# The S5 kernel matrix of a hybrid decoder block, stored with the group outside

## The chip, the cores and the metric

One core of a Trainium2 chip runs the whole block in one launch. The metric is the device time of that launch in microseconds (us). The kernel before took 2400.34 us, the median of three runs (2392.76 to 2401.52).

## The reference, cut to what matters

The block has two parallel heads behind a modulated RMSNorm (an S5 state-space group and a sparse-attention group), an output projection and a gated MLP. Only the S5 part is touched. With `u` of shape (1, 512, 1024) in float32:

```
uf = u.reshape(bsz, seq, 64, 16)                 # 64 groups of 16 channels
dt = exp(log_dt); ab = exp(lam * dt)             # complex, 64 states a group
bb = f * b                                       # f from ab and lam
bu = einsum('bsgh,gph->sbgp', uf, bb)            # complex
states = associative_scan(a * s + bu)            # over the 512 positions
y = Re(einsum('sbgp,ghp->bsgh', states, c)) + d_skip * uf
z = gelu(y); out = z * sigmoid(z @ w_glu + b_glu)
```

The kernel computes the scan in chunks of 8 positions: 512 positions are 64 chunks (index `j`), each with 8 offsets (index `l`). Inside a chunk the output is a product with a small matrix that depends only on the distance between two offsets, the S5 kernel; what comes from earlier chunks goes through a state that is scanned over the 64 chunks.

## The kernel before, in words

The work is tiled in 128 partitions by 512 positions. Phase A multiplies the input with the first weight slices; phase B1 (`phase_b1`) runs twelve further projections (`proj`, 48 matmuls each in three float32 parts), and among them eight *octets* (`s5_octet`), each the S5 work for 8 of the 64 groups. Then come attention, the GLU, the output projection and the MLP.

In an octet VectorE builds the tables `w1`, `TT`, `C`, `Sn`; TensorE transposes `w1` into `W1` (L567, copied by ScalarE at L568) and multiplies the 8 x 16 columns of the S5 kernel (L575). ScalarE copies these into `Kt` (L577): 16 partitions (the input channel `i`) by 1024 elements, stored as `x g` with `x` = 16 times the distance plus the output channel, and the group `g` inside, so that the copy writes every eighth element. VectorE adds `d_skip` at the last 16 `x` (L580). POOL's DMA queue stores `Kt` to the DRAM tensor `k_s` (L581), where a row is 15 x 128 elements: 1024 of the matrix and 896 zeros, which one DMA fills during phase A (L278). A second DMA of POOL (L585) reads the rows back shifted, row `i` for offset `l` from element 128 `l` on, 1024 contiguous elements for each of the 128 partitions. That makes the block-triangular matrix `w3`, in the profile the tile s5w; there is one buffer of it.

Meanwhile a row of the weights is multiplied with a shift vector (s5wt, L593, loaded by SP's queue) for the bias of `U` (tile s5U, L601 to L604). TensorE multiplies `W1` with `U` (L608), VectorE scans over the chunks (L615 to L618), TensorE swaps halves with a constant matrix (L621), and VectorE finishes the state `SS` (L624 to L626). At the end stands what the prediction calls the Y block, for each of the 8 groups one matmul with `w3[:, :, g]` (L630) and one with `TT[:, g]` (L631), both 64 columns wide and into one accumulator. ScalarE applies gelu (L634) and POOL stores the result to `z_d` (L635).

```
for g in range(8):
    T.matmul(Y[:, 64 * g:64 * g + 64], w3[:, :, g], U[:, g], start=True, stop=False)
    T.matmul(Y[:, 64 * g:64 * g + 64], TT[:, g, 0:8].rearrange("p k h -> p (k h)"), SS[:, g, 0:64],
             start=False, stop=True)
```

Each engine works off its own queue in order. No order is written out by hand: a planner lays the queues out when the program is built, from the order of the code, its priorities (`hp()` lifts the S5 work of TensorE) and estimated durations, so the matmuls of an octet stand among those of the projections.

Of the kernel before, what the change touches and what calls it, by code (L numbers as in the profile page):

```python
# [10 lines left out]
F32 = mybir.dt.float32  # L11
# [7 lines left out]
P = 128  # L19
# [32 lines left out]
class Block:  # L52
# [143 lines left out]
    def phase_a(self, hh, hl, tab, ps):  # L196


        nc, tc, a, V, A, T = self.nc, self.tc, self.a, self.V, self.A, self.T
        m, b = self.mod, self.mad  # L200
        with ExitStack() as st:
            pa = st.enter_context(tc.tile_pool(name="pa", bufs=1))
# [18 lines left out]
            with tc.tile_pool(name="s5p", bufs=1) as pp:  # L221
                pu = [ps.tile([P, S], F32, name="b", bufs=8) for _ in range(8)]
                for kt in range(KT):
                    asc = pa.tile([P, 2], F32, name="asc", bufs=4)
                    first = self.ada(1, kt, asc[:, 0:1 if kt else 2], pw, 3)
# [11 lines left out]
                    x = xt[kt]  # L237
# [23 lines left out]
            for kt in range(KT):  # L261
                ash = pa.tile([P, 1], F32, name="ash", bufs=4)
                self.ada(0, kt, ash, pw, 3)
                wh, wl = self.slices(a["wk"], kt)
                V.tensor_add(m[:, 0, kt:kt + 1], ash, b[:, 0, kt:kt + 1])
                if kt >= 8:
                    hl[kt] = tab.tile([P, S], F32R, name=f"hl{kt}")
                self.modulate(xt[kt], m[:, 1, kt:kt + 1], m[:, 0, kt:kt + 1], rb, hh[kt], hl[kt], pa)
                if kt < 8:
                    V.tensor_mul(us[kt], us[kt], rp)  # L270
                if kt == 4:
                    self.rot = tab.tile([P, 2, S], F32, name="rot")
                    nc.sync.dma_start(self.rot.rearrange("p a s -> p (a s)"), a["cons"][:, C_COS:])
                if kt == 1:

                    zero = pa.tile([P, P], F32, name="zero")
                    nc.gpsimd.memset(zero, 0.0)
                    self.after([nc.gpsimd.dma_start(  # L278
                        self.k_s.rearrange("o i x -> (o i) x")[:, 1024:].rearrange("p (a b) -> p a b", b=P),
                        zero.unsqueeze(1).to_broadcast([P, 7, P]))], first)  # L280
                if 2 <= kt < 10:
                    nc.sync.dma_start(self.u_d[kt - 2].rearrange("l p j -> p l j"), us[kt - 2])
                h = hh[kt], hl[kt]
                for i in range(4):
                    self.mm3(pk[i], (wh[:, i], wl[:, i]), h, kt == 0, kt == KT - 1)
                v = [w[:, 4:8].rearrange("p a m -> p (a m)") for w in (wh, wl)]
                for t in range(4):
                    self.mm3(pk[4 + t], [x[:, P * t:P * t + P] for x in h], v, kt == 0, kt == KT - 1)
            def tmp(n):
                return pw.tile([P, 2048], F32, name="adw", bufs=3)[:, 0:S * n].rearrange("p (a s) -> p a s", s=S)  # L290

            for i in range(4):
                p = pk[i]
                if i == 0:
                    q, t = (pa.tile([P, 8, 64], F32, name="modt", bufs=2).rearrange("p a b -> p (a b)")
                            for _ in range(2))
                    p = self.rope(p, q, t, self.rot[:, 0], self.rot[:, 1], 64)
                if i % 2 == 0:
                    o = tmp(4).bitcast(F32R)
                self.spill(self.qk_d[0, P * i:P * i + P], p, o[:, 2 * (i % 2):2 * (i % 2) + 2])  # L300
            o = tmp(4)
# [188 lines left out]
    def s5_octet(self, o, Tb, W, ps):  # L490

        nc, V, A, T, a = self.nc, self.V, self.A, self.T, self.a
# [3 lines left out]
        U, bc = self.s5_next  # L496
# [66 lines left out]
        with hp():  # L563
            for q in range(2):
                p = ps.tile([P, 4, P], F32, name="tp", bufs=2)
# [1 line left out]
                    T.transpose(p[:, g], w1[:, 4 * q + g].rearrange("p r i -> p (r i)"), self.ident)  # L567
                A.copy(W1[:, 4 * q:4 * q + 4], p)  # L568
        Kt = W.tile([P, 8, 9 * 16], F32, name="s5bg", bufs=3).rearrange("p a b -> p (a b)")
        Kt = Kt[:16, 0:1024].rearrange("p (x g) -> p x g", g=8)  # L570
        with hp():
            for q in range(2):
                p = ps.tile([P, 4, P], F32, name="tp", bufs=2)
                for g in range(4):
                    T.matmul(p[:16, g], bb[:, 0, 4 * q + g], TT[:, 4 * q + g, 1:9].rearrange("p k h -> p (k h)"),  # L575
                             start=True, stop=True)
                A.copy(Kt[:, :, 4 * q:4 * q + 4].rearrange("p x g -> p g x"), p[:16])  # L577
        dd = W.tile([16, 16, 8], F32, name="s5dd")
        nc.sync.dma_start(dd, a["s5d"][:, o])
        V.tensor_add(Kt[:, 112:], Kt[:, 112:], dd)  # L580
        nc.gpsimd.dma_start(self.k_s[o, :, 0:1024].rearrange("i (x g) -> i x g", g=8), Kt)  # L581
        w3 = W.tile([P, P, 8], F32, name="s5w3")

        src = self.k_s[o]
        nc.gpsimd.dma_start(w3.rearrange("p x g -> p (x g)"),  # L585
                            bass.AP(src.tensor, src.offset, [[P, 8], [15 * P, 16], [1, 1024]]))


        bu = W.tile([P, 2], F32, name="bu", bufs=2)
# [9 lines left out]
        with hp():  # L599
            p = ps.tile([P, S], F32, name="acc", bufs=4)  # L600
# [26 lines left out]
        with hp():  # L627
            Y = ps.tile([P, S], F32, name="acc", bufs=4)
            for g in range(8):
                T.matmul(Y[:, 64 * g:64 * g + 64], w3[:, :, g], U[:, g], start=True, stop=False)  # L630
                T.matmul(Y[:, 64 * g:64 * g + 64], TT[:, g, 0:8].rearrange("p k h -> p (k h)"), SS[:, g, 0:64],  # L631
                         start=False, stop=True)
            zz = W.tile([P, 8, 64], F32, name="s5x", bufs=4)
            A.activation(zz.rearrange("p g j -> p (g j)"), Y, AF.Gelu_apprx_tanh)  # L634
            nc.gpsimd.dma_start(self.z_d[o].rearrange("(h g) l j -> l h g j", g=8), zz)  # L635
# [853 lines left out]
```

## Time and profile before

| | before |
|---|---|
| median of the runs (lowest, highest) | 2400.34 us (2392.76, 2401.52) |
| the profiled execution | 2398.66 us |
| its span, first to last instruction | 2396.9 us |
| mean granted TensorE clock | 0.963 |
| TensorE matmul / weight load busy | 2244.6 us (94%) / 1967.3 us (82%) |
| VectorE, ScalarE, POOL busy | 1865.8 us (78%), 1084.3 us (45%), 288.5 us (12%) |
| DMA packets, bytes | 92370, 398.17 MB |

The busy time of TensorE counts matmuls, whose ends are modelled; weight loads run beside them and are listed apart (PEld). A float32 matmul of 128x128 weights appears as two records, so 64 matmuls of a line are "x128". [...]

### The profile page before, as it was taken

Reading aid. Unit: us, or ns where it says so; the run is one execution under the profiler, and the core shown is the slowest. Engines: PE = TensorE matmul, PEld = TensorE weight load, DVE = VectorE, ACT = ScalarE, POOL = GpSimd, SP = SyncE. Lnnn points to the kernel's source line nnn. Section 1 sums busy time; section 2 is a strip of 40 time slices with the busy share of each in tenths; the row PEclk is TensorE's granted clock in tenths of the full one; section 3 lists DMA queues with packets and bytes.
Section 4 is the critical chain, followed back from the end, with each engine's and each line's share of the span. In section 5 each row is a group of like instructions: output and inputs, shape, how many; then the busy total and the mean of one; then the engine's idle time right before and its main releaser. Section 6 shows DMA issues by size and latency. Waiting matters only on the chain.

```text
span 2396.9 us, 34691 instructions
## 1 busy us (share of the span) xinstructions
PE 2244.6 (94%) x13694; PEld 1967.3 (82%) x13694; DVE 1865.8 (78%) x2776; ACT 1084.3 (45%) x1807; POOL 288.5 (12%) x375
## 2 busy tenths in 40 slices
PE   7778999989899879899999999999999899999997
PEld 5666787866677667889999999999999788888887
DVE  7789877749988878889999999999999685433436
ACT  3322444448867742644444444444444322221215
POOL 7996110100000011000000000000000000000000
PEclk9989998979999889999999999999999999999999
DMA  9666744676576567233333333333332684323223
GB/s 339 255 223 215 235 146 140 186 207 195 174 233 218 186 251 289 101 120 119 119 119 119 119 119 119 120 119 119 119 119 102 243 322 182 139 90 126 101 88 106
DMA packets 92370, 398.17 MB, mean 166 GB/s; under 512 B 19776, under 2 KB 28352, under 8 KB 56240
## 3 DMA queue, kind: packets, MB, share of 16 engines
q1 hardware_dynamic: 77856, 344.60, 41.6%
q0 software_dynamic: 14352, 51.36, 6.1%
q8 instruction: 107, 1.75, 0.3%
q14 instruction: 55, 0.45, 0.1%
HBM read 358.20 MB, written 37.69 MB: 165 GB/s over the span
## 4 chain that ended last, share of the span: by engine, by line
PE 71%; DVE 11%; issue 6%; POOL 5%; ACT 4%; DMA 3%; SPq 0%; POOLq 0%; DVEq 0%; ACTq 0%
PE dn L88 7%; PE dn L87 7%; PE dn L89 7%; PE sa L89 7%; PE sa L87 7%; PE sa L88 7%; PE sb L87 5%; PE sb L89 5%; PE sb L88 5%; PE mm L87 2%; PE mm L89 2%; PE mm L88 2%; DVE wl L62 2%; DVE adw L111 1%; PE s L870 1%
## 5 line engine op out<-in xcount | busy, mean ns | idle before, releaser
L62 ACT CAST wh<-wr 128x1024 fp32r<-128x1024 f32 (+1 forms) x257 | 261.9, 1024 | 519.7 <-PE dn L88 331.6
L62 DVE TENSOR_TENSOR wl<-wr,wh 128x1024 fp32r<-128x1024 f32 (+1 forms) x255 | 307.2, 1209 | 68.6 <-ACT wh L62 47.7
L87 PE MATMUL dn<-ah,wh 128*128 128x512 f32 (+1 forms) x704 | 274.9, 391 | 7.6 <-ACT ah L62 7.6
L88 PE MATMUL dn<-al,wh 128*128 128x512 f32 (+1 forms) x704 | 278.0, 395 | 0.0
L89 PE MATMUL dn<-ah,wl 128*128 128x512 f32 (+1 forms) x704 | 273.3, 388 | 0.0
L1249 DVE SCALAR_TENSOR_TENSOR x<-dn,mod,x 128x512 f32<-128x512 f32 (+1 forms) x104 | 73.2, 707 | 203.4 <-PE dn L89 202.8
L87 PEld LDWEIGHTS dn<-ah,wh 128*128 128x128 f32 x704 | 132.8, 189 | 40.8 <-ACT ah L62 7.8
L89 PEld LDWEIGHTS dn<-ah,wl 128*128 128x128 f32 x704 | 132.7, 189 | 30.3
L111 DVE SCALAR_TENSOR_TENSOR adw<-adw,silc 128x2048 f32<-128x2048 f32 x63 | 147.9, 2348 | 12.1 <-DMA adw<-in_wada_dram 11.8
L88 PEld LDWEIGHTS dn<-al,wh 128*128 128x128 f32 x704 | 132.8, 189 | 29.6 <-DVE al L62 0.4
L87 PE MATMUL mm<-yh,wh 128*128 128x512 f32 (+1 forms) x320 | 130.4, 412 | 22.5 <-DVE x L1026 7.2
L62 ACT CAST wh<-wq 128x1024 fp32r<-128x1024 f32 x84 | 88.0, 1048 | 137.6 <-DVE wq L1193 101.0
L62 ACT CAST xh<-wq 128x1024 fp32r<-128x1024 f32 x84 | 88.5, 1054 | 135.8 <-DVE wq L1193 100.8
L88 PE MATMUL mm<-yl,wh 128*128 128x512 f32 (+1 forms) x320 | 129.7, 406 | 3.9 <-DVE yl L62 3.9
L1082 POOL DMA_DIRECT2D a_d<-cv x44 | 23.9, 543 | 879.4 <-DVE cv L1081 879.4
L89 PE MATMUL mm<-yh,wl 128*128 128x512 f32 (+1 forms) x320 | 129.1, 405 | 0.3 <-DVE wl L62 0.3
L62 DVE TENSOR_TENSOR wl<-wq,wh 128x1024 fp32r<-128x1024 f32 x84 | 102.4, 1220 | 33.1 <-ACT wh L62 33.1
L62 DVE TENSOR_TENSOR xl<-wq,xh 128x1024 fp32r<-128x1024 f32 x84 | 102.5, 1220 | 31.4 <-ACT xh L62 31.4
L1193 DVE TENSOR_TENSOR wq<-wq,wr 128x1024 f32<-128x1024 f32 x84 | 102.1, 1216 | 0.1
L87 PEld LDWEIGHTS mm<-yh,wh 128*128 128x128 f32 x320 | 63.0, 199 | 37.7 <-issue 12.3
L87 PE MATMUL b<-hh,wh 128*128 128x512 f32 x192 | 67.3, 408 | 23.6 <-ACT hh L238 16.4
L62 ACT CAST xh<-wr 128x1024 fp32r<-128x1024 f32 x63 | 65.8, 1044 | 47.0 <-issue 19.9
(525 smaller groups left out, 7207.3 us busy)
## 6 DMA issues: line engine op xcount, KB each, us to landing
adw<-in_wada_dram SPq DMA_DIRECT2D x49, 1024.0 KB, 7.0
wr<-in_wup_dram SPq DMA_DIRECT2D x46, 1024.0 KB, 4.9
wq<-in_wup_dram SPq DMA_DIRECT2D x42, 1024.0 KB, 6.6
wr<-in_wdn_dram SPq DMA_DIRECT2D x40, 1024.0 KB, 4.9
wr<-in_wada_dram SPq DMA_DIRECT2D x32, 1024.0 KB, 4.9
wr<-in_wout_dram SPq DMA_DIRECT2D x16, 1024.0 KB, 5.8
adw<-in_wada_dram POOLq DMA_DIRECT2D x14, 1024.0 KB, 6.9
wr<-in_wp_dram SPq DMA_DIRECT2D x12, 1024.0 KB, 5.6
```

What stands on the lines that cost most here:

```text
L62: return self.A.copy(hi, src), self.V.tensor_sub(lo, src, hi.bitcast(F32))
L87: self.T.matmul(ps, wh, xh, start=start, stop=False)
L88: self.T.matmul(ps, wh, xl, start=False, stop=False)
L89: self.T.matmul(ps, wl, xh, start=False, stop=stop)
L111: self.V.scalar_tensor_tensor(t, t, 1.0, self.silc, op0=ALU.mult, op1=ALU.mult, accum_out=out)
L870: T.matmul(s[:, :c + n], q[hd], K[b][:, i, k0:k0 + c + n], start=i == 0, stop=i == 1)
L1082: self.nc.gpsimd.dma_start(self.a_d[:, m], val)
L1193: V.tensor_add(src, src, add)
L1249: V.scalar_tensor_tensor(x, p, self.mod[:, 5, m:m + 1], x, op0=ALU.mult, op1=ALU.add)
```

## The change

The group moves outside. In DRAM a row of `k_s` becomes 8 pieces of 240 elements, one per group: 128 of the matrix and 112 zeros. `Kt` becomes `g x`, so that the copy at L577 writes contiguous elements; the addition reads `dd` with the group rearranged. The store writes 8 pieces of 128 elements (512 bytes) in each of 16 rows in place of one of 1024. The load of `w3` reads 8 pieces of 128 elements in each of 128 partitions in place of one of 1024, and the shift from one offset `l` to the next is 16 elements. The zero fill writes 8 pieces of 112 elements in each of 128 rows in place of 7 x 128. The weight tile of L630 is `w3[:, g]`, 128 contiguous elements a partition.

```
-                    zero = pa.tile([P, P], F32, name="zero")
+                    zero = pa.tile([P, 112], F32, name="zero")
...
-                        self.k_s.rearrange("o i x -> (o i) x")[:, 1024:].rearrange("p (a b) -> p a b", b=P),
-                        zero.unsqueeze(1).to_broadcast([P, 7, P]))], first)
+                        self.k_s.rearrange("o i (g x) -> (o i) g x", g=8)[:, :, P:],
+                        zero.unsqueeze(1).to_broadcast([P, 8, 112]))], first)
...
-        Kt = Kt[:16, 0:1024].rearrange("p (x g) -> p x g", g=8)
+        Kt = Kt[:16, 0:1024].rearrange("p (g x) -> p g x", g=8)
...
-                A.copy(Kt[:, :, 4 * q:4 * q + 4].rearrange("p x g -> p g x"), p[:16])
+                A.copy(Kt[:, 4 * q:4 * q + 4], p[:16])
...
-        V.tensor_add(Kt[:, 112:], Kt[:, 112:], dd)
-        nc.gpsimd.dma_start(self.k_s[o, :, 0:1024].rearrange("i (x g) -> i x g", g=8), Kt)
-        w3 = W.tile([P, P, 8], F32, name="s5w3")
+        V.tensor_add(Kt[:, :, 112:], Kt[:, :, 112:], dd.rearrange("p x g -> p g x"))
+        nc.gpsimd.dma_start(self.k_s[o].rearrange("i (g x) -> i g x", g=8)[:, :, 0:P], Kt)
+        w3 = W.tile([P, 8, P], F32, name="s5w3")
...
-        nc.gpsimd.dma_start(w3.rearrange("p x g -> p (x g)"),
-                            bass.AP(src.tensor, src.offset, [[P, 8], [15 * P, 16], [1, 1024]]))
+        nc.gpsimd.dma_start(w3, bass.AP(src.tensor, src.offset, [[16, 8], [15 * P, 16], [15 * 16, 8], [1, P]]))
...
-                T.matmul(Y[:, 64 * g:64 * g + 64], w3[:, :, g], U[:, g], start=True, stop=False)
+                T.matmul(Y[:, 64 * g:64 * g + 64], w3[:, g], U[:, g], start=True, stop=False)
```

## Rows read from the trace of the kernel before

**Rows 1.** Busy time by stretch: PE, PEld, DVE, ACT, POOL, clock, DMA share, GB/s.

```profile
280.00:485.00 205.00, 199.67 (x1006) 167.39 (x1005) 159.28 (x271) 93.44 (x184) 20.96 (x30) 0.94 0.53 154
```

**Rows 2.** Instructions on the accumulator: min/median/max ns, first and last start, form.

```profile
L608 PEld LDWEIGHTS acc<-s5U,s5W x128: 186/192/333, 280.4 to 491.9; 128*128 128x128 f32 x128
L630 PEld LDWEIGHTS acc<-s5U,s5w x128: 312/314/337, 293.0 to 511.5; 128*128 128x128 f32 x128
L630 PE MATMUL acc<-s5U,s5w x128: 219/398/451, 293.4 to 511.6; 128*128 128x64 f32 x128
```

**Rows 3.** TensorE's timeline (start, duration), Y block of octet 0; a dense L608 stretch.

```profile
298.32 0.39 PE L631 MATMUL acc<-s5SS,s5TT 128*128 128x64 f32 x2
298.55 0.64 PE L630 MATMUL acc<-s5U,s5w 128*128 128x64 f32 x2
...
302.49 0.39 PE L631 MATMUL acc<-s5SS,s5TT 128*128 128x64 f32 x2
...
430.61 0.55 PE L608 MATMUL acc<-s5U,s5W 128*128 128x64 f32 x4
430.97 0.48 PE L89 MATMUL mm<-hh,wl 128*128 128x512 f32 x1
```

**Rows 4.** Waits, 232 to 525 us (sum, times, longest); VectorE's timeline behind octet 0.

```profile
DVE s5x L546 <- issue: 21.0, 6, 4.3
PE acc L601 <- DVE bg L597: 3.3, 2, 3.0
302.93 0.64 DVE L546 TENSOR_TENSOR s5x<-s5SH,s5SB 128x256 f32<-128x256 f32 x1 [4.33 <-issue]
```

**Rows 5.** TensorE's timeline in octet 1; stretches: busy, clock, DMA share, GB/s.

```profile
324.52 0.66 PE L630 MATMUL acc<-s5U,s5w 128*128 128x64 f32 x2
...
325.40 0.66 PE L630 MATMUL acc<-s5U,s5w 128*128 128x64 f32 x2
...
324.00:330.00 6.00, 6.00 (x23) 0.50 0.40 101
392.00:395.00 3.00, 3.00 (x10) 0.52 0.36 93
450.00:453.00 3.00, 3.00 (x10) 0.52 0.34 92
511.00:523.00 12.00, 7.45 (x34) 0.52 0.63 197
```

**Rows 6.** ScalarE's copies from PSUM: min/median/max ns, first and last start, form.

```profile
L577 ACT COPY s5bg<-tp x16: 1093/1164/1283, 269.6 to 473.0; 16x512 f32<-16x512 f32 x16
L568 ACT COPY s5W<-tp x16: 586/588/593, 261.1 to 470.4; 128x512 f32<-128x512 f32 x16
```

**Rows 7.** POOL's DMAs, each line's duration and landing; last the zero fill's landing.

```profile
L585 POOL DMA_DIRECT2D s5w<-k_s x8: 615/728/830, 276.8 to 484.1; - x8
DMA to landing us min/median/max: 6.6/8.0/9.2
...
L635 POOL DMA_DIRECT2D z_d<-s5x x8: 1292/1320/1332, 303.8 to 513.4; - x8
DMA to landing us min/median/max: 5.7/6.5/9.6
...
k_s<-zero POOLq DMA_DIRECT2D x1, 448.0 KB, 3.9
```

**Rows 8.** Timelines of POOL and TensorE: w3 load and first use, octets 1, 5.

```profile
302.95 0.61 POOL L585 DMA_DIRECT2D s5w<-k_s  x1 [12.61 <-PE acc L631]
...
316.83 0.45 PE L630 MATMUL acc<-s5U,s5w 128*128 128x64 f32 x2
...
427.50 0.82 POOL L585 DMA_DIRECT2D s5w<-k_s  x1
...
442.31 0.45 PE L630 MATMUL acc<-s5U,s5w 128*128 128x64 f32 x2
```

## The prediction, made before the changed kernel ran

> **What bounds the kernel now.** I read the stretches first, then the forms of instruction in the stretch that the change touches, then its timeline, and last who waits there. The S5 octets lie between 232 and 515 us, among twelve projections. In the middle of that, from 280 to 485 us, TensorE is busy for 199.67 of 205 us, VectorE for 159.28 and ScalarE for 93.44; the DMA engines are at 0.53 [rows 1]. So TensorE sets the pace there, and its queue is in order: a microsecond taken out of it moves everything behind it forward, as long as no other wait ends later.
>
> In each of the eight octets TensorE runs one "Y block": the line with `w3` (L630) alternates with L631, eight times each, both with a 128x128 float32 weight tile, 64 moving columns and two records per matmul. Yet a weight load of L630 takes 314 ns at the median and one of L608 192, though both have the same moving tile s5U; the matmul of L630 gets longer with its load, to 398 ns [rows 2]. What sets L630 apart is how its weights lie: `w3[:, :, g]` steps 32 bytes from element to element, those of L608 and L631 are packed. The timeline gives the pace. In octet 0 an L631 starts at 298.32, the next L630 at 298.55, and six pairs later, at 302.49, the last L631: 0.695 us a pair, 0.23 of them for L631 and 0.465 for L630. Four packed L608 records in a row take 430.97 - 430.61 = 0.36 us [rows 3].
>
> VectorE is held by the same blocks: before L546, in six octets, it stands still for 21.0 us in sum, and it restarts as the block ends (302.93 in octet 0) [rows 4]. So the Y block is on the path whichever of the two engines one follows.
>
> **The change, part by part.**
>
> *Weight loads of `w3` (the gain).* After the change `w3[:, g]` is packed as W1 and TT are. A block holds seven L630-L631 pairs behind its first L631, so there are 56 of them; 6 ran at the low clock (three in octet 1, one each in octets 3, 5 and 7) and 50 at the full one. Ends for a packed pair at full clock: 0.36 us if it runs like the four dense L608 records, 0.46 if L630 only gets as fast as L631 is beside it now (2 x 0.23) [rows 3]. I take 0.39, nearer to the dense run, since the whole block becomes a dense run of packed loads. 50 x (0.695 - 0.39) = 15.2 us (ends 11.8 and 16.8). The eighth L630 of each octet stands alone behind L621, where its load is mostly covered: 0 to 0.15 us each, 0.6 us in sum.
>
> [...]
>
> *Clock.* [...] But the clock fell inside the Y blocks of octets 1, 3, 5 and 7, in their later part each time, and stayed down for some 6, 3 and 3 us in the first three [rows 5]; in the other four octets it did not fall. A block of some 3 us in place of 5 may be over before it falls. If it never fell there: 6 x (0.88 - 0.39) = 2.9 us, and of the 12 low microseconds about 9 lie behind the blocks and would take half as long, 4.5 us, together 7.4. If nothing changes, 0; if the clock falls once more elsewhere, as in octet 1, 3 us lost. I take 3.6 us, the middle of the first two.
>
> *Copies into Kt (L577).* Their output becomes packed: 1164 ns would become 588, as L568 takes for 512 elements a partition [rows 6]. 16 x 0.58 = 9.2 us less on ScalarE, which is busy less than half of the time. Little of it lies on the path; where such a copy stands ahead of the E2 copies that VectorE waits for, it counts. I take 0.5 us (ends 0 and 3).
>
> *The addition of dd (L580)* keeps its 128 elements in 16 partitions; its strides move from one operand to the other. Nothing, within 0.3 us an octet either way, on an engine with 46 us free [rows 1].
>
> *The store of Kt and the load of w3.* The bytes stay (64 and 512 KB); the pieces become 512 bytes, 128 in place of 16 in the store and 1024 in place of 128 in the load. Both are issued on POOL's queue, which is nearly empty. The nearest row with 1024 pieces is the z_d store, of 256 bytes each: POOL holds it for 1320 ns and it lands in 5.7 to 9.6 us; the w3 load now takes 728 ns and lands in 6.6 to 9.2 [rows 7]. So POOL gets about 8 x 0.6 us more, ahead of z_d stores and q spills whose readers are far off. What hides the landing: octet 1 is tightest, issued at 302.95, when the Y block of octet 0 frees the single w3 buffer, and first used at 316.83, 13.9 us later; octet 5 has 427.50 to 442.31, 14.8 us [rows 8]; the other six have more. I expect 8 to 12 us and so nothing on the path; the bad end is the third rival.
>
> *The zero fill (L278)* writes the same 448 KB at 124 us, in 1024 pieces of 448 bytes in place of 896 of 512, for readers after 276 us. It lands in 3.9 us now [rows 7]; even at twice that it is hidden from them, and for the loads beside it I allow 0 to 1 us. [...]
>
> *What is late next.* With TensorE some 19 us ahead, its own waits grow, as the one for VectorE before L601 (3.3 us in two octets now) [rows 4]. VectorE has 159 us of work in 205 us, and its pauses shrink with the blocks, so most of the gain stays. I take 3 us off (ends 1 and 7).
>
> Sum: 15.2 + 0.6 + 3.6 + 0.5 - 3 = 16.9, say 17 us. The profiled execution took 2398.66 us (a span of 2396.9 and 1.8 around it), which becomes 2382; the median of the runs, 2400.34, is 1.7 above it, so the forecast is **2383 us**. Its own range is 2375 (dense pairs, a clock that no longer falls and little returned: 16.8 + 0.6 + 7.4 + 0.5 = 25) to 2388 (no help from the clock: 13).
>
> **Rivals.**
>
> 1. *Half is given back.* Pairs end at 0.46 us, the clock falls as before, and the queues, which a planner orders by estimated durations of these very DMAs and copies, come out in an order that leaves TensorE waiting more: 11.8 us less some 3 gives 9, so 2391. For it: VectorE is next in line after the blocks. Against: in 205 us TensorE idles only 5.3 now [rows 1].
>
> [...]
>
> 3. *The load of w3 comes late.* TensorE's queue stops at the first L630 of an octet, and all projections stand behind it. In octets 1 and 5 that begins at landings of 13.9 and 14.8 us [rows 8]; each microsecond beyond costs two, and from about 17 us on, where the other octets join, five and more. At 17 us it costs 3.1 + 2.2 there and some 1 elsewhere, at 19 about 16, all of the gain; at 21 about 29, and the time is 2412. So it decides from about twice today's landing. For it: eight times as many pieces, behind a store that is cut up too. Against: the z_d store with as many pieces lands within 9.6 us [rows 7].
>
> **Chances.** Forecast 0.60; first rival 0.26; load no faster 0.06; late load 0.08. A difference of 0.5%, 12 us, is about what a measurement of this kernel can tell from no change. Faster than 2388.3: the forecast and a little of the first rival, 0.62. Within 12 us: the rest of the first, the second and a mild third, 0.31. Slower: 0.07. The range that leaves two in ten out goes from 2374 through most of the first rival to 2396.
>
> **What would show it.** Right: L630's weight load near 190 ns and its matmul near 275; pairs in the Y block 0.36 to 0.46 us apart; L577 near 590 ns; VectorE's wait at L546 shorter by about 2 us an octet; no wait of TensorE for s5w; fewer low-clock stretches among the octets; and the phases behind the octets as long as before. Wrong: a wait of TensorE for the w3 load, pairs still 0.69 apart, or a gain in the octets that is lost again before the end of the program.

## The result, and the profile after

The changed kernel takes 2380.18 us at the median of 11 runs (2369.43 to 2392.75) beside 2395.31 us for the kernel before (11 runs, 2388.89 to 2401.52): a ratio of 0.9942, 95% interval 0.9926 to 0.9958. That is 14 us less by the ratio and 15 by the medians, against 17 forecast. The time lies 3 us under the predicted 2383, in part because the forecast started from 2400.34 us, the median of three runs, and eleven runs of the same kernel give 5 us less. A second set of runs (experiment 5) gave 0.9934 (0.9912 to 0.9956). The profiled execution has a span of 2378.4 us, 18.5 less than the one before.

Below the changed line L585 every line number is one lower than before: the `w3` matmul is L629, the TT matmul L630, the swap matmul of `z3` L620, the bias matmul of `ub` L600, the weighted sum of `s5wt` L592. L546, L514, L577 and L585 keep theirs. With line numbers and shapes set aside, the two traces show the same order of instructions on TensorE, ScalarE, POOL and SyncE; on VectorE one MEMSET comes one place later in this profile, and in the second profile of the changed kernel (experiment 5) it stands where it stood before. So what differs is time alone.

Instructions on the weight tile in the changed kernel (min/median/max ns, first and last start, form), which answer to [rows 2]:

```profile
L629 PEld LDWEIGHTS acc<-s5U,s5w x128: 190/192/337, 294.1 to 494.3; 128*128 128x128 f32 x128
L629 PE MATMUL acc<-s5U,s5w x128: 219/275/421, 294.6 to 494.4; 128*128 128x64 f32 x128
```

The load fell from 314 to 192 ns, to the value of the packed L608, and the matmul from 398 to 275. TensorE's timeline of the Y block of octet 1 (start, duration), beside [rows 3]:

```profile
327.25 0.33 PE L630 MATMUL acc<-s5SS,s5TT 128*128 128x64 f32 x2
327.42 0.39 PE L629 MATMUL acc<-s5U,s5w 128*128 128x64 f32 x2
327.64 0.39 PE L630 MATMUL acc<-s5SS,s5TT 128*128 128x64 f32 x2
...
330.32 0.39 PE L630 MATMUL acc<-s5SS,s5TT 128*128 128x64 f32 x2
```

Seven pairs take 330.32 - 327.25 = 3.07 us, 0.44 us a pair: each matmul now follows the last after 0.22 us, the pace that L631 alone had before. The six blocks behind it take 3.07 to 3.17 us; only that of octet 0, at the low clock, takes 5.98. Before, the eight took 4.81 to 5.18.

Busy time and granted clock (as a share of full speed) by stretch in the changed kernel (columns as in [rows 1]); the first row answers to [rows 1], the second is new, the third to fifth answer to low stretches of [rows 5]:

```profile
280.00:485.00 205.00, 196.14 (x1061) 160.16 (x1060) 166.18 (x283) 94.95 (x205) 27.75 (x31) 0.95 0.63 173
...
294.50:311.00 16.50, 16.50 (x66) 15.09 (x65) 7.97 (x17) 5.46 (x15) 2.64 (x2) 0.51 0.14 41
324.00:330.00 6.00, 6.00 (x41) 5.30 (x39) 5.11 (x13) 0.57 (x1) 0.55 (x1) 1.00 0.44 112
392.00:395.00 3.00, 2.94 (x16) 2.07 (x15) 3.00 (x5) 1.61 (x5) 0.00 (x0) 1.00 0.85 197
450.00:453.00 3.00, 3.00 (x21) 2.52 (x20) 3.00 (x3) 1.98 (x8) 0.00 (x0) 1.00 1.00 326
```

The clock no longer falls inside the Y blocks, where before it stood at 0.50 to 0.52. But a new low stretch of 17 us (294.9 to 312.0, granted 0.50) has come around octet 0's block; in the 16.5 us of the row TensorE is busy throughout and has 66 records, where the kernel before, at full clock, had 91 in the same 16.5 us.

Waits of the changed kernel between 232 and 525 us (sum, times, longest); the first answers to [rows 4]:

```profile
DVE s5x L546 <- issue: 14.5, 6, 8.1
...
DVE s5bc L514 <- DMA s5bc<-in_s5bc_dram: 2.7, 1, 2.7
...
PE acc L620 <- DVE bu L595: 1.9, 1, 1.9
...
PE acc L600 <- DVE bg L596: 1.6, 2, 1.0
```

VectorE's wait at L546 fell from 21.0 to 14.5 us, and 8.1 of what is left is the one slow block of octet 0; the other five waits went from 16.7 to 6.4, the 2 us an octet that the prediction named as a sign. No row has TensorE waiting for the tile of `w3`. New is a wait of VectorE for coefficients, `s5bc`. The copies and the load, beside [rows 6] and [rows 7]:

```profile
L577 ACT COPY s5bg<-tp x16: 571/576/578, 269.3 to 459.2; 16x512 f32<-16x512 f32 x16
```

```profile
L585 POOL DMA_DIRECT2D s5w<-k_s x8: 1328/1332/1373, 278.0 to 468.4; - x8
...
DMA to landing us min/median/max: 8.6/9.3/11.6
```

The copies halved, 1164 to 576 ns. The load holds POOL for 1332 ns in place of 728 and lands in 9.3 us in place of 8.0. Octet 1's `w3` was loaded at 307.87 [rows 8: 302.95] and first used at 323.58, 15.7 us later; the shortest such distance is now octet 5's, 13.6 us, so the landing of at most 11.6 us was covered.

**Where the 18.5 us came from.** Taking the end of each Y block as a mark: octet 0's ends at 307.36 (302.49 before), so the kernel is 4.9 us late there. From there to the end of octet 7's block it needs 187.13 us in place of 209.34, 22.2 less: 12.5 in the seven blocks themselves, 9.7 between them. Behind octet 7 it gains another 1.2. The 9.7 are 6.0 between the blocks of octets 2 and 3, 2.3, 1.3 and 1.7 behind the blocks of octets 1, 3 and 5, and 1.7 lost behind octet 0. So the net of this one pair of profiles is two gains and a loss, and the experiments were made to part them.

### The profile page after: what moved, and what is told of

It is laid out like the page before. It is cut to its first block, busy times and chain, and to the rows that moved or that the text cites. A ratio compares the mean times of both kernels' runs of the same rounds, so it can differ in the third digit from the quotient of the medians.

```text
span 2378.4 us, 34691 instructions
## 1 busy us (share of the span) xinstructions
PE 2227.8 (94%) x13694; PEld 1949.1 (82%) x13694; DVE 1866.3 (78%) x2776; ACT 1076.5 (45%) x1807; POOL 290.6 (12%) x375
## 4 chain that ended last, share of the span: by engine, by line
PE 70%; DVE 11%; issue 6%; POOL 5%; ACT 4%; DMA 3%; SPq 0%; POOLq 0%; DVEq 0%; ACTq 0%
PE dn L87 7%; PE dn L89 7%; PE dn L88 7%; PE sa L89 7%; PE sa L87 7%; PE sa L88 7%; PE sb L87 5%; PE sb L89 5%; PE sb L88 5%; PE mm L87 2%; PE mm L89 2%; PE mm L88 2%; POOL stt L338 2%; DVE wl L62 2%; DVE adw L111 1%
## 5 line engine op out<-in xcount | busy, mean ns | idle before, releaser
L62 ACT CAST wh<-wr 128x1024 fp32r<-128x1024 f32 (+1 forms) x257 | 262.0, 1024 | 522.5 <-PE dn L88 323.0
L133 POOL TENSOR_TENSOR rms_r<-rms_v,mhalf 128x2 f32<-128x2 f32 (+1 forms) x8 | 8.9, 1106 | 641.7 <-DVE rms_v L131 641.7
```

Of the source, the lines that this page charges most:

```text
L62: return self.A.copy(hi, src), self.V.tensor_sub(lo, src, hi.bitcast(F32))
L133: self.rms_pow = self.nc.gpsimd.tensor_tensor(r[:, 0:n], v[:, 0:n], self.mhalf.to_broadcast([P, n]), op=ALU.pow)
```

## The experiments

In 1, 2, 3, 4, 6, 7 and 10 the weights' values come in another order than the reference needs; shapes and counts are the same.

**1. Only the weights' stride undone.** The changed kernel, its tile filled as in the change, read with a step of eight elements:

```
-T.matmul(Y[...], w3[:, g], ...)
+T.matmul(Y[...], w3 as (x g)[:, :, g], ...)
```

> The changed kernel, but the w3 matmul reads its weight tile with a step of eight elements again (so the S5 output is another one); DMA pieces and Kt copies stay as changed, and every engine's queue has the same order. Theory (the packed weight loads carry the gain): weight loads back at 314 ns, Y-block pairs at 0.69 us, and the time within 5 us of the kernel before (ratio 0.998 to 1.001). Rival (the shorter ScalarE copies carry it): the time stays near the changed kernel, ratio 0.994 to 0.996, although the loads are slow.

2397.61 us (12 runs) beside 2394.84, ratio 1.0005 (0.9986 to 1.0025). The loads are back at 334 ns, and the whole gain is gone, though the copies into Kt stay packed. The granted clock falls to half again at the end of four Y blocks (330.6, 357.9, 422.8 and 480.8 us, 3.4 us each; means over 4 us of 0.60 to 0.84 there).

**2. Only the weights packed.** The kernel before, same transfers, same Kt, the tile read as if the group were outside:

```
-T.matmul(Y[...], w3[:, :, g], ...)
+T.matmul(Y[...], w3 as (g x)[:, g], ...)
```

> The kernel before, but the w3 matmul reads 128 contiguous elements as its weight tile (so the S5 output is another one); DMAs and Kt copies as before, queues in the same order. Theory (packed loads): pairs at 0.45 us and most of the gain, 11 to 15 us, ratio 0.994 to 0.9955. Rival (ScalarE copies): under 5 us, ratio above 0.998.

2372.86 us, ratio 0.9894 (0.9872 to 0.9915): 22 us under the kernel before, more than the 11 to 15 expected and more than the whole change gave. So something in the rest of the change costs.

**3. The packed copies added to it.** As the second, and the copies L577 write Kt packed too; both transfers stay in 4096-byte runs.

```
+Kg = Kt as (g x)
-A.copy(Kt[:, :, 4*q:4*q+4] ..., p[:16])
+A.copy(Kg[:, 4*q:4*q+4], p[:16])
```

> The kernel before with packed weight tiles and packed Kt copies, but with the store and load of the matrix in 4096-byte runs as before (so the S5 output is another one): all of the change but the small DMA pieces. Theory (the pieces are hidden): like the changed kernel, ratio 0.993 to 0.9955, the w3 load landing in 8 us and POOL holding it for 0.73 us. Rival (the pieces cost time on the path): faster than the changed kernel by 4 us or more, ratio below 0.9925.

2371.49 us, ratio 0.989 (0.9865 to 0.9916), the same as without: 9 us less on ScalarE are worth nothing that can be measured. The ratio is the one expected of the rival (below 0.9925), by which the small pieces cost time on the path.

**4. A ladder of steps.** In one block the eight `w3` matmuls read weights that step by 1, 2, ..., 8 elements of four bytes.

```
-T.matmul(Y[group g], w3[:, g], ...)
+T.matmul(Y[group g], w3 with a step of g + 1 elements, ...)
```

> The changed kernel with the eight w3 matmuls of an octet on eight lines, the weight tile of group g read with a step of g+1 elements (4 to 32 bytes; the S5 output is another one). Theory (the cost comes from how many elements share a short stretch of SBUF): loads near 190 ns up to a step of two to four elements, then rising to 314 at eight. Rival (any step but one is slow): all steps from two on near 314 ns. Time: between the kernel before and the changed one, 2382 to 2395.

One run, 2386.82 us. The loads by step, 1 at the top and 8 at the bottom (min/median/max ns):

```profile
L637 PEld LDWEIGHTS acc<-s5U,s5w x16: 187/190/190, 293.8 to 491.7; 128*128 128x128 f32 x16
...
L639 PEld LDWEIGHTS acc<-s5U,s5w x16: 196/197/198, 299.8 to 497.4; 128*128 128x128 f32 x16
...
L641 PEld LDWEIGHTS acc<-s5U,s5w x16: 252/257/263, 300.2 to 497.9; 128*128 128x128 f32 x16
...
L643 PEld LDWEIGHTS acc<-s5U,s5w x16: 309/319/332, 300.8 to 498.6; 128*128 128x128 f32 x16
...
L651 PEld LDWEIGHTS acc<-s5U,s5w x16: 312/334/336, 303.5 to 501.2; 128*128 128x128 f32 x16
```

Step 2 is nearly free (197 ns against 190), step 3 takes a third longer (257), 4 to 8 take 306 to 334 ns: the rise is over at four, where the theory put it as far as eight. The runs give the time by step alone; the cause that the theory names is not shown.

**5 to 7. The pieces, on one chip.** The fifth is the changed kernel again; the sixth is the third with the load alone cut into 512-byte pieces; the seventh is the changed kernel with the load alone in 4096-byte runs, its store and its zero fill still in pieces.

```
# sixth: from whole runs to pieces; seventh: the other way
-bass.AP(src.tensor, src.offset, [[P, 8], [15 * P, 16], [1, 1024]])
+bass.AP(src.tensor, src.offset, [[16, 8], [15 * P, 16], [15 * 16, 8], [1, P]])
```

> The changed kernel once more, for a second profile beside the next three. Theory (its small DMA pieces cost some 10 us, by holding up the s5bc load of the next octet in octet 0, so that VectorE and then TensorE stop and the clock falls): ratio 0.993 to 0.996 again, and again VectorE waits over 2 us for s5bc near 285 us and the clock is low around 300. Rival (that profile was a chance event, and the first comparison ran under other conditions): ratio near 0.990, no such wait.

> The kernel with packed weights, packed Kt copies and the old store and zero fill, but the w3 load in 1024 pieces of 512 bytes as in the change (the S5 output is another one). Theory (the load's pieces cost): slower than the same kernel with the load in 4096-byte runs, ratio 0.993 to 0.996 against 0.989. Rival (the store's or the zero fill's pieces cost): ratio 0.988 to 0.991.

> The changed kernel, but with the w3 load in 4096-byte runs (the S5 output is another one): store and zero fill stay in small pieces. Theory (the load's pieces cost): ratio 0.988 to 0.991. Rival (store or zero fill): 0.993 to 0.996.

Beside 2391.6 us for the kernel before: 2374.65 (0.9934, 0.9912 to 0.9956), 2374.41 (0.9928, 0.9903 to 0.9953) and 2366.14 (0.9895, 0.987 to 0.9919). With the load in pieces 17 us are gained, with the load in whole runs 25, whatever the store and the zero fill look like. So the load's pieces cost some 8 us here, and the store's and the fill's nothing that shows. The intervals overlap slightly (0.9912 against 0.9919), but eleven of the twelve runs of the fifth and sixth kernels take 2373.05 us or more, and five of the seventh's six 2368.26 or less. With the slow weight loads of the first experiment no such cost shows: 1.0005 with an upper bound of 1.0025, where 8 us would be 1.0033.

How they cost shows in octet 0. The rows below are TensorE's timeline ahead of the swap matmul of octet 0 (in brackets: idle before, and what ended it), first of the changed kernel, then of the sixth and the seventh:

```profile
293.60 1.12 PE L620 MATMUL acc<-s5x,cons 128*128 128x512 f32 x2 [1.94 <-DVE bu L595]
```

```profile
292.90 1.13 PE L622 MATMUL acc<-s5x,cons 128*128 128x512 f32 x2 [2.99 <-DVE bu L597]
```

```profile
290.14 1.13 PE L621 MATMUL acc<-s5x,cons 128*128 128x512 f32 x2 [0.53 <-DVE bu L596]
```

VectorE is late for `bu` in the first two because it stood still a few microseconds earlier. VectorE's timeline of the changed kernel, and then the issues of the two loads in question there, from SP's and POOL's timelines:

```profile
287.62 0.29 DVE L514 TENSOR_SCALAR s5bc<-s5bc,cons 128x128 f32<-128x128 f32 x1 [2.69 <-DMA s5bc<-in_s5bc_dram]
```

```profile
280.88 0.33 SPq L485 DMA_DIRECT2D s5bc<-in_s5bc_dram  x1
```

```profile
277.97 1.34 POOL L585 DMA_DIRECT2D s5w<-k_s  x1 [5.90 <-DMA k_s<-s5bg]
```

The load of coefficients (octet 3's) is issued 2.9 us behind the first `w3` load and is in flight beside it. Its landing in the changed kernel, then in the seventh:

```profile
DMA to landing us min/median/max: 6.7/6.7/6.7
```

```profile
DMA to landing us min/median/max: 4.1/4.1/4.1
```

Over all kernels that load it, this one transfer lands in 4.8 to 7.2 us beside a cut-up `w3` load (changed, 1, 4, 5, 6, 8, 11) and in 2.8 to 4.1 beside one in whole runs (before, 2, 3, 7, 12). In the sixth kernel VectorE waited 3.10 us at this place, in the seventh not at all. The fifth, the same program as the changed kernel, kept the ratio but not what was expected of its trace: VectorE waited 0.72 us there, not over 2, and the clock did not fall around 300 us. After the longer pauses, in the changed kernel and the sixth, TensorE's clock fell (0.51 from 294.5 to 311 us; 0.58 and 0.56 in the two stretches of 2 us from 294 to 298); in the seventh it stayed up through the same stretch (columns as in [rows 1]):

```profile
291.00:308.00 17.00, 16.73 (x102) 14.23 (x101) 14.09 (x24) 10.93 (x24) 2.48 (x3) 1.00 0.47 138
```

**8. Groups in twos.** The layout keeps two groups interleaved: weights step by 2, pieces of 1024 bytes.

```
-w3 = W.tile([P, 8, P], F32, name="s5w3")
+w3 = W.tile([P, 4, P, 2], F32, name="s5w3")
-... [[16, 8], [15 * P, 16], [15 * 16, 8], [1, P]]
+... [[32, 8], [15 * P, 16], [15 * 32, 4], [1, 2 * P]]
```

> A kernel that computes the block as before: groups stored in pairs, so that the w3 load and the store move 1024-byte pieces (512 in the load), the zero fill 896-byte ones, and a weight tile is read with a step of two elements, which the ladder timed at 197 ns against 190. Theory (fewer, longer pieces cost about half as much): ratio 0.990 to 0.993, faster than the changed kernel; pairs at 0.46 us. Rival (any piece under 4096 bytes costs the same): ratio 0.994 to 0.996.

2374.76 us, ratio 0.9923 (0.99 to 0.9945), beside the fifth's 2374.65: halving the number of pieces won nothing back that these runs can tell, against the theory, which had it faster than the changed kernel. Its blocks take 3.15 to 3.27 us, and it pauses at both places (2.08 and 2.85 us, below).

**9 and 10. The coefficients' loads taken away,** with the `w3` load in pieces and in whole runs.

```
-bc = W.tile(..., name="s5bc", bufs=2)
-nc.sync.dma_start(bc, a["s5bc"][:, o])
+if o < 2: (the same two lines, the tile kept)
+bc = self.bcs[o % 2]
```

> The changed kernel with the coefficients (s5bc) loaded for octets 0 and 1 alone; later octets use these two tiles, so they compute with other coefficients, and six loads of 256 KB are left out. The weights' load stays in 512-byte pieces. Theory A (the pieces cost time by holding back the load of the coefficients, for which VectorE waited 0.7 to 3.1 us): with these loads gone nothing is left to hold back, and this kernel is within 3 us of the next one, which loads in 4096-byte runs; against the kernel before some 0.990 or lower, and VectorE waits for no coefficients. Theory B (the pieces cost by another way: other transfers, or the pool engine's longer hold): this kernel is still 6 to 10 us slower than the next.

> As the run before, with the weights' load in 4096-byte runs (the weights' values come in another order). Theory A: equal to the run before within 3 us, ratio some 0.989. Theory B: 6 to 10 us faster than the run before. Either way not much under the store-in-pieces run (0.9895), since there nothing waited for the coefficients: more than 4 us under would say that these loads cost time on their own.

2372.44 us (0.9912, 0.9888 to 0.9936) and 2368.34 (0.9895, 0.9872 to 0.9917). The difference of 4.1 us lies between the two theories, and the intervals overlap, so it decides for neither. The pause at octet 0 is shorter (1.15 us, 0.50 with whole runs), as theory A has it, and VectorE waits for no coefficients there. But these two profiles differ at a second place, ahead of the bias matmul of octet 3. Ninth kernel, waits between 280 and 485 us, TensorE's timeline, and the stretch behind it:

```profile
DVE s5wt L595 <- DMA s5wt<-in_wuT_dram: 4.7, 3, 2.2
```

```profile
360.31 0.39 PE L603 MATMUL acc<-bg,cons 128*128 128x8 f32 x2 [2.68 <-DVE bg L599]
```

```profile
360.00:371.00 11.00, 10.69 (x46) 9.23 (x47) 7.54 (x10) 4.56 (x14) 0.57 (x1) 0.69 0.81 210
```

The same three views of the tenth:

```profile
DVE s5wt L596 <- DMA s5wt<-in_wuT_dram: 2.6, 2, 2.1
```

```profile
356.78 0.39 PE L604 MATMUL acc<-bg,cons 128*128 128x8 f32 x2 [1.08 <-DVE bg L600]
```

```profile
357.00:368.00 11.00, 10.88 (x67) 8.64 (x67) 9.70 (x11) 6.63 (x16) 0.57 (x1) 1.00 0.71 201
```

Here it is an `s5wt` load that VectorE waits for (2.18 us, until 356.40). But no `w3` load was in flight beside it. The issues of that `s5wt` load and of octet 3's `w3` in the ninth kernel, from SP's and POOL's timelines:

```profile
349.51 0.33 SPq L594 DMA_DIRECT2D s5wt<-in_wuT_dram  x1
```

```profile
357.63 1.33 POOL L588 DMA_DIRECT2D s5w<-k_s  x1 [6.69 <-PE mm L88]
```

Octet 2's `w3`, issued at 323.80, had landed in 9.3 us. In all eleven kernels of the table below this `s5wt` load has landed before octet 3's `w3` load is issued, and it takes 5.2 to 7.1 us with whole runs and 5.3 to 7.0 with a cut-up load. So what holds it back is not the pieces of `w3` in flight beside it, and the cause stays open. The kernel before had this second pause too, and the fall behind it; its timeline and stretch:

```profile
369.12 0.60 PE L601 MATMUL acc<-bg,cons 128*128 128x8 f32 x2 [2.95 <-DVE bg L597]
```

```profile
368.00:378.00 10.00, 8.88 (x32) 7.91 (x33) 5.74 (x7) 3.35 (x11) 0.56 (x1) 0.51 0.89 265
```

Set side by side, the two places in eleven profiles (pause of TensorE in us, and where the granted clock was low right behind it):

| kernel | load of w3 | swap matmul, octet 0 | low behind it | bias matmul, octet 3 | low behind it |
|---|---|---|---|---|---|
| before | whole | 0.80 | no | 2.95 | 368–378 |
| 2 | whole | 0.84 | no | 2.69 | 363–367 |
| 3 | whole | 0.76 | no | 1.00 | no |
| 7 | whole | 0.53 | no | 1.18 | no |
| 10 | whole | 0.50 | no | 1.08 | no |
| changed | pieces | 1.94 | 295–312 | 1.03 | no |
| changed again (5) | pieces | 0.78 | no | 1.73 | 363–370 |
| 1 | pieces | 2.64 | 293–310 | 0.46 | no |
| 6 | pieces | 2.99 | 294–298 | 1.08 | no |
| 8 | 1024 bytes | 2.08 | 293–296 | 2.85 | 361–371 |
| 9 | pieces | 1.15 | no | 2.68 | 362–369 |

At the first place only kernels with a cut-up load have the long pause and the fall, four of six; at the second both kinds have them, three of six and two of five. Of the kernels left out of the table, the ladder (4, pieces) has 2.61 us and a fall (295 to 298) at the first place, 0.12 and none at the second; the eleventh (pieces) 1.66 and 4.04 us and a fall at both; the twelfth (whole runs) 2.62 us at the first place and no fall behind it, as its timeline and the stretch show:

```profile
295.53 1.13 PE L621 MATMUL acc<-s5x,cons 128*128 128x512 f32 x2 [2.62 <-DVE bu L596]
```

```profile
293.00:311.00 18.00, 15.47 (x95) 13.32 (x96) 16.17 (x31) 10.89 (x23) 3.00 (x4) 1.00 0.51 149
```

So a long pause is mostly, not always, followed by a fall. Where there is one, pause and fall cost 3 to 7 us together: between the blocks of octets 2 and 3 from end to end the third, seventh and tenth kernels take 30.5 to 30.8 us, those with a fall there 33.7 (2), 34.6 (5), 35.5 (9), 37.1 (8) and 38.4 (before, 1.8 of it for its strided block). Each profile is one execution, and the fifth shows that the same program can have its pause at either place. Over the whole stretch, from where TensorE stops ahead of octet 0's swap matmul to the last TT matmul of octet 7, the five profiles with a cut-up load and weights packed or two elements apart (changed, 5, 6, 8, 9) take 199.7 to 204.0 us, the four with whole runs and packed weights (2, 3, 7, 10) 191.8 to 198.5.

**11. The `w3` half of the block first.** The changed kernel, all eight `w3` matmuls ahead of the eight TT matmuls:

```
 for g in range(8):
-    T.matmul(..., w3[:, g], ..., start=True, stop=False)
+    T.matmul(..., w3[:, g], ..., start=g == 0, stop=False)
+for g in range(8):
     T.matmul(..., TT[...], ..., start=False, stop=g == 7)
```

> The changed kernel, with the Y block in another order: the eight w3 matmuls first, then the eight TT matmuls, each half accumulating into the same tile. The w3 half needs only U and w3, so it can run while VectorE still works out SS. If TensorE stands waiting for SS ahead of the Y block and nothing else is there to run, this takes up to 8 x 0.11 us off each octet's chain, some 5 to 7 us in all, ratio some 0.990; if TensorE fills that wait with other matmuls anyway, nothing is won, ratio 0.993; a loss of several us if the w3 half pushes the other matmuls that run there.

2377.4 us, ratio 0.993 (0.9909 to 0.995): nothing won. TensorE waits longer for `bg` (5.2 us in five waits, 1.6 in two for the changed kernel), and its profile has low stretches at both places (294 to 308 and 366 to 376 us; mean granted clock 0.94 from 280 to 485), so the time does not price the order by itself.

**12. Whole runs and packed weights, by a copy on the chip.** The kernel before, its load landing in another tile and copied to the packed one by ScalarE:

```
-nc.gpsimd.dma_start(w3 as (x g), ...)
+nc.gpsimd.dma_start(raw, ...)
+A.copy(w3, raw.rearrange("p (x g) -> p g x", g=8))
```

> The kernel before, with k_s and its two transfers as they were (group inside, 4096-byte runs); the load lands in a tile of the s5bg slots, and one ScalarE copy of 128x1024 an octet writes it with the group outside into the weight tile, so that the weights are contiguous and no transfer is in 512-byte pieces. The two 16x512 copies of L577 and L568 took 0.58 us packed and 1.16 us with a step, so a copy of twice the length should take some 1.2 to 2.4 us, 10 to 19 us of ScalarE in a stretch where it is busy 95 of 205 us. If these hide: ratio 0.989 as with packed weights and whole runs, 8 us under the changed kernel. If ScalarE stands waiting for the load (its landing is 7 to 9 us) with the next layer's casts behind it, TensorE waits for those casts: 1 to 2 us an octet, ratio 0.993 to 0.997. More than 0.9975 would say that the third s5bg slot's longer use holds back VectorE.

2395.18 us, ratio 1.0024 (1.0005 to 1.0043). The copy (min/median/max ns), and ScalarE's wait for the load:

```profile
L627 ACT COPY s5w<-s5bg x8: 2025/2163/2262, 284.6 to 496.3; 128x1024 f32<-128x1024 f32 x8
```

```profile
ACT s5w L627 <- DMA s5bg<-k_s: 22.3, 5, 5.7
```

The copies are 17 us on an engine that has that room; but five waits, 22.3 us, stand in an in-order queue which also carries the bias and swap copies for TensorE, and the gain is gone, as the second of the expected cases has it, and more. In octet 3 ScalarE waits 5.59 us for the load, and TensorE then stands 4.42 us, until 369.50, for the biased `U` that comes behind the copy; two more such waits of TensorE for ScalarE take 3.17 and 4.21 us, and low stretches of 6.8 us begin at 369.5, 403.6 and 468.4 (granted clock 0.50 to 0.70 as means over 4 us). The ratio is also over the 0.9975 that was to say that the longer use of the third s5bg slot holds back VectorE; the trace has one such wait, 2.8 us. So whole runs and packed weights, the 25 us of the seventh kernel, were not brought together this way.

## Why the prediction was right, step by step

**The Y block.** That its weight loads set the pace, and that packing removes it, is shown by the first two experiments (1.0005 with the step back, 0.9894 with packed weights alone) and by the 192 ns. The size was off: the pace is 0.44 us a pair, near the end of the range (0.46) and not at 0.39. The four dense L608 records stand right behind a 512-column matmul, and a packed matmul in that place is followed sooner than one in a run: in the kernel before the next one starts 0.17 us behind the L608 at 297.46, whose load began at 297.23 while the 512-column matmul of 297.15 ran (0.48 us); in the changed block each starts 0.22 us behind the last. No run tests why. The eighth L630 had its load mostly covered, as taken: in octet 0 of the kernel before it lasted from 293.02 to 293.76, the swap matmul in front of it from 292.48 to 293.60. Over eight blocks the third kernel saves 39.15 - 24.85 = 14.3 us, low pairs included, where 15.2 were taken at the full clock and up to 2.9 more for the low pairs.

**The load that is no faster,** 0.06 of the chances, falls: the median went from 314 to 192 ns, and the tile was written by a DMA in both kernels. In the ladder, loads of the same 128 columns took 190 to 334 ns at the median.

**The clock.** The part that was seen came in full: behind the blocks of octets 1, 3 and 5 the changed kernel gains 2.3 + 1.3 + 1.7 = 5.3 us (4.5 was the best case), and none of the blocks 1 to 7 holds a fall. It is no chance of one profile: all nine profiles with weights packed or two elements apart (changed, 2, 3, 5 to 10) take 20.8 to 20.9, 26.6 and 26.9 us from these blocks' ends to the next blocks, against 23.2, 27.9 and 28.6 before. What was missed is the low stretch of the kernel before at 368 us. It lies in no Y block, and it came with a 2.95 us pause; I read that wait only as a thing that would grow. Without it 6.0 us came between octets 2 and 3 in the profiled execution. But four of these nine profiles (2, 5, 8, 9) have a fall there and five have none, so these 6.0 us are not shown to be the change's. The term was undersized: 3.6 taken with the low pairs in it, 5.3 measured behind the blocks alone. Its 0.88 us for a low pair is the distance of the two L630 in [rows 5]; the packed block of octet 0, at the low clock too, took 5.98 / 7 = 0.85.

**The copies and the addition.** 0.5 us taken for L577, nothing that can be told from zero measured (2372.86 us without and 2371.49 with packed copies, experiments 2 and 3), as ScalarE's share said.

**The pieces.** "And so nothing on the path" is the step that failed. The landing, 9.3 us, is inside the 8 to 12 expected, and no wait for `w3` came up, so the third rival in its own form is out too. I asked only who waits for this load, and not whose loads are in flight beside it. One was VectorE's `s5bc` of octet 3, which landed in 4.8 to 7.2 us beside a cut-up load and in 2.8 to 4.1 beside whole runs; VectorE waited 0.7 to 3.1 us for it, where with whole runs it waited not at all, TensorE paused for VectorE, and in six of these seven profiles the clock fell. The median over all eight `s5bc` loads is 4.7 to 5.2 us in the changed kernel, 5, 6 and 8, and 4.0 to 4.2 in 2, 3 and 7; that of the `s5wt` loads does not tell the two kinds in the table apart (3.9 to 4.4 and 4.1 to 4.3). The price was some 8 us on one chip (17 against 25); the 4 of experiments 9 and 10 lie within their noise.

**What is late next.** 3 us taken; TensorE's idle time from 280 to 485 us went from 5.3 to 8.9 us, 3.5 more. With store and fill in pieces and the load in whole runs (7) it is 7.7.

**The sum.** 23 us for packing (experiments 2 and 3: 22 and 23) less 8 for the pieces is 15, and 17 was forecast: an undersized gain and an unseen cost nearly cancelled, so that the time came out right is in part luck. Blocks and clock behind them, 14.3 + 5.3, account for 20 of the 23; the rest has no place of its own in the rows. The first rival was near in the pace (0.46 for 0.44) but its cause, reordered queues, did not occur.

What stays open: the 8 us are the difference of medians whose intervals overlap slightly, and the rows account for them by place only for the executions profiled; the pause and the fall at octet 0 are not all of it, since the fifth kernel's profiled execution had neither at that size (0.78 us, and its fall at the second place) and still took 2374.41 us, the middle of its runs. No run shows on which DMA engines, or in what order, the pieces of the two loads went. A version with two `w3` tiles, which would move the load, was not run.

## What to carry to other kernels

Weights that a matmul loads should lie packed, or at most two fp32 elements apart (190 and 197 ns here); with 64 moving columns a matmul took 0.465 us with a step of eight and 0.22 packed. Before cutting a transfer into smaller pieces, list not only its reader but every load in flight beside it and who waits for those. And read each low-clock stretch back to what stood ahead of it, here a pause of TensorE or a block of slow weight loads: the fall behind a pause can cost more than the pause (1.94 us of pause and 17 us at granted 0.50 behind it in the changed kernel). A fall that one profile shows can be absent from the next execution of the same program (295 to 312 us in the changed kernel, none there in experiment 5), so take a second profile before counting it as a gain or a loss.

## What was not expected of the hardware

- A weight load of 128x128 fp32 took 190, 197, 257 and 319 ns at steps of 1, 2, 3 and 4 elements, and 306 to 334 at 4 to 8: little further cost beyond four.
- A load of 512 KB in 1024 pieces of 512 bytes landed only 1.3 us later than in 128 of 4096 (9.3 against 8.0 us), yet the program with packed weights lost some 8 us by it; store and zero fill in pieces cost nothing that could be measured.
- Pauses of TensorE of 1.7 to 3.0 us at the two places were followed by some 3 to 17 us at about half clock in all nine cases of the table (granted 0.50 from 295 to 312 us in the changed kernel, 0.51 from 368 to 378 in the one before); the thirteen of 0.5 to 1.2 us there were not. It is no rule: the twelfth kernel's 2.62 us at the first place was not followed by a fall, and a pause of 2.3 us near 260 us goes with a low stretch in the kernel before, the changed one, 2, 3, 5, 6, 9 and 10 (0.50 to 0.66 from 260 to 264 us) and with none in 7, 8 and 12 (1.00).
- A ScalarE copy of 128x1024 fp32 read with a step of 32 bytes took 2163 ns, against 576 to 588 for packed ones of 512.
